# A hybrid encoder step on one core: low weight parts moved to VectorE, layer norm as two interleaved instructions a tile, output weights in pieces of 512

## The chip, the core and the metric

The kernel runs on one core of a Trainium2 chip. The metric is the device time of one execution in microseconds (us), taken as the median of several runs. Five engines work at once, each through its own instructions in a fixed order: TensorE (PE; its weight loads are PEld), VectorE (DVE), ScalarE (ACT), GpSimd (POOL) and SyncE (SP), which here issues the DMAs.

## What is computed

One layer of a streaming encoder for 2048 prompt tokens and 8 x 16 sample tokens (17 tiles of 128 tokens, 1024 features). All in float32, cut to what matters here:

```
h = RMSNorm(x);  u, v, zA, q, k, vv, zB, qi, ki, wi, gA, gB = split(h @ w_in)      # 1024 x 5704
vn   = LayerNorm(gelu(v)) * ln_g + ln_b                                             # 512 wide
a    = gelu(u) * (w_s @ vn + b_s) * silu(zA)                                        # per 128 tokens, 8 groups
score[q, l] = sum over 8 heads of relu(qi . ki) * wi;  keep the 256 best keys of each query
b    = softmax attention over the kept keys * silu(zB)
m    = sigmoid(gA) * (a @ w_pa) + sigmoid(gB) * (b @ w_pb)
y    = RMSNorm(x + m @ w_out)                                                       # 1024 x 1024
```

## The kernel before

Every matmul operand is held as two float32r numbers, a high part and a low part (`wh` and `wl`, `hh` and `hl`), and a product is three matmuls: high x high, high x low, low x high (`mm3`, line 170). The high part is made by ScalarE (`split_hi`, line 176), the low part, which is raw minus high, by `split_lo` (line 179) on the engine it is given.

**Weights.** `load_w` (line 140) brings a weight of 1024 rows and 128, 256 or 292 columns in chunks: SyncE issues a DMA into a staging tile `ws` (one buffer), ScalarE makes `wh`, GpSimd makes `wl` (one subtraction for the whole chunk: 128x1024, 128x512 or 128x1168), and the staging tile is free for the next DMA. `wh` and `wl` have two buffers, so one weight is prepared while the one before it is used. Only the very first weight has its low part made by VectorE.

**Order of the stages.** Tokens are worked on in two halves (9 tiles, then 8). `phase_p1` makes keys, values and queries; `phase_p2` makes mixer A: v in two pieces of 256 columns (`pairs`, gelu into `vn`), layer norm, u, the gate of mixer B, the spatial products (line 400) that read `vn`, and in the end the merge gates. Beside these the selection runs: `weave` takes steps of it between the steps of the main work. It has two lanes, each with its own query tile: `scores` (lines 504 to 511: two matmuls into a bank `ps_ix` of which there are two, ScalarE's relu into `r` with two buffers, VectorE's multiply-add into `s`), then 31 rounds of counting (line 581 on VectorE, line 591 on ScalarE) with small instructions on one number a partition (lines 592, 596, 597), then the mask (lines 623 to 632). This woven stage lies between about 245 us and 1445 us. Then `phase_b` is attention, and `phase_c` makes m and the output. Tile's scheduler fixes the order of each engine's instructions beforehand by its own simulated times; on the chip each engine keeps to it.

**Layer norm** (lines 371 to 385): after both pieces of v, per tile `bn_stats` and `bn_aggr` on VectorE; one Newton step for all tiles; then per tile one `tensor_scalar` on VectorE (line 381: minus mean, times factor) and two `tensor_tensor` on GpSimd (lines 382 and 383: times ln_g, plus ln_b).

**Output.** `phase_c` cuts `w_out` into four weights of 256 columns (`split_w`, tiles `wo0h` to `wo3l`), loaded in pieces while the first group is merged. `out` (line 987) makes a tile's 1024 columns as two banks of 512, and each bank as two sums of 24 matmuls with 256 moving columns (line 996).

Of the kernel before, what the change touches and what calls it, by code (L numbers as in the profile page):

```python
# [17 lines left out]
P = 128  # L18
# [39 lines left out]
def encoder_step(ctx: ExitStack, tc: tile.TileContext, x_prompt, x_sample, cache_k, cache_v, cache_kidx,  # L58
# [24 lines left out]
    class Banks:  # L83
        """PSUM, a bank a tile: how many banks each use has."""
# [30 lines left out]
    # scratch in DRAM  # L115
# [14 lines left out]
    def out_rows(prompt, sample, t, pat):  # L130
        """Token rows of tile t of an output [1, ...] as [128, width]."""
# [5 lines left out]
    # ---------------------------------------------------------------- weights  # L137
    WS_BUFS = 1

    def load_w(srcs, beside=False, eng=nc.gpsimd, stage=None):  # L140
        """Columns of weights as exact float32r pairs, [128, rows / 128, width] high and low: ranges of columns
        beside or below each other."""
# [5 lines left out]
        for below in ([srcs] if beside else [[s] for s in srcs]):  # L148
            n = below[0].shape[0] // P
            step = min(n, 1024 // width if width <= 256 else 4)  # L150
            for k in range(0, n, step):
# [9 lines left out]
                split_lo(wl[:, o], raw, wh[:, o], eng)  # L161
# [3 lines left out]
    def mm3(out, lh, ll, rh, rl, nk, cost):  # L165
        """Sum over nk of l[k]^T r[k] from float32r pairs, in steps."""
# [14 lines left out]
    def rsqrt(out, root, v):  # L181
        """1 / sqrt(v) from about sqrt(v), by a Newton step; root is lost."""
# [6 lines left out]
    def rms_scale(pool, x, out, g, inv=None, known=False, parts=1):  # L189
        """RMSNorm; inv keeps the factor."""  # L190
# [16 lines left out]
    # ---------------------------------------------------------------- phase A  # L207
# [5 lines left out]
    class Normed:  # L213
        """The transposed RMSNorm(x) of a half's tokens as float32r pairs, by group."""
# [5 lines left out]
        def ahead(self, n):  # L220
            """Loads and scales the rows of the next n tiles."""
# [48 lines left out]
    def phase_p1(half, hT, p1, wa, at_queries=None):  # L270
        """Keys, values, queries and the indexer's."""
        gs = HALVES[half]
        gids = [GROUP_OF[g[0]][0] for g in gs]
        # k | ki | wi | v
# [25 lines left out]
        for c, dst in ((C_QI, qi_s), (C_Q, q_s)):  # L300
            for b in range(2):
# [3 lines left out]
                for j in range(2):  # L305
                    for gid in gids:
# [3 lines left out]
                        sb = p1.tile([P, 512], F32, tag="ev", name="ev", bufs=3)  # L310
# [5 lines left out]

    def phase_p2(half, hT, at_gates=None):
        """Mixer A and its part of the merge; the gates of mixer B."""
# [832 lines left out]
```

## Time and profile before

| | |
|---|---|
| median of 3 runs | 2239.65 us (2237.88 to 2241.37) |
| profiled execution, span from first to last instruction | 2240.6 us (its own time is not listed apart from the runs) |
| PE busy | 2150.1 us, 96% |
| DVE busy | 1649.8 us, 74% |
| ACT busy | 1207.6 us, 54% |
| POOL busy | 567.2 us, 25% |
| chain that ended last | PE 63%, DVE 19%, DMA 6%, ACT 5% |

The profile is of one execution. Busy time counts an instruction from start to end; the matmuls of TensorE overlap each other, so its useful rate is read from the distance between starts, not from the busy share. The granted clock (PEclk) is a share of 2.4 GHz: 0.50 is the lower of its two levels, 1.2 GHz. "idle before" is time for which the engine had no instruction under way, with what ended it.

### The profile page before, as it was taken

The numbers are of one execution on the slowest core, as the hardware profiler recorded it, in microseconds if no ns is written. First come the engines' busy times: TensorE is split into PE (matmuls) and PEld (weight loads), VectorE is DVE, ScalarE is ACT, GpSimd is POOL, SyncE is SP. The second block draws the span as 40 slices with busy tenths as digits, with TensorE's granted clock in tenths as the row PEclk, the third lists the DMA queues.
The fourth block names the chain that finished last, engine by engine and source line by source line (L and its number), as shares of the span: only waits on it lengthen the run. The fifth ranks groups of instructions, "written<-read, shape, count | busy, mean of one in ns | idle before, by whom it ended". The sixth has DMA issues, their size and how long they took to land.

```text
span 2240.6 us, 39567 instructions
## 1 busy us (share of the span) xinstructions
PE 2150.1 (96%) x14712; PEld 2066.3 (92%) x14712; DVE 1649.8 (74%) x4034; ACT 1207.6 (54%) x2181; POOL 567.2 (25%) x437
## 2 busy tenths in 40 slices
PE   7999999899999999979998999999999999999998
PEld 7999999799999998979998999878899999989998
DVE  6205879998898897998988796578777788855343
ACT  5225646465565554545664654277766577743121
POOL 1121121432132121151123121132354423243000
PEclk9999999899999999999999999999999999999999
DMA  6333333123153233211223222553344421054341
GB/s 199 100 105 109 90 93 88 50 71 94 36 165 89 71 88 114 74 45 55 84 79 100 78 80 79 131 142 98 101 144 124 137 79 39 15 172 153 119 150 67
DMA packets 251008, 218.90 MB, mean 98 GB/s; under 512 B 46528, under 2 KB 238656, under 8 KB 250816
## 3 DMA queue, kind: packets, MB, share of 16 engines
q1 hardware_dynamic: 250816, 216.39, 32.7%
q8 instruction: 115, 1.88, 0.3%
q14 instruction: 77, 0.63, 0.1%
HBM read 152.45 MB, written 63.81 MB: 97 GB/s over the span
## 4 chain that ended last, share of the span: by engine, by line
PE 63%; DVE 19%; DMA 6%; ACT 5%; issue 4%; POOL 2%; SPq 1%; ACTq 0%; DVEq 0%; POOLq 0%
PE ps_mm L170 40%; DVE junk L581 5%; PE ps_po L747 5%; DVE s L511 4%; PE ps_tr L730 4%; PE ps_mm L706 2%; DVE bc L597 2%; PE ps_mm L707 2%; PE ps_ix L170 2%; ACT junk L591 2%; PE ps_ix L504 2%; PE ps_ix L505 1%; DMA ws<-in_w_in_dram 1%; DMA q<-q_s 1%; DVE vn L381 1%
## 5 line engine op out<-in xcount | busy, mean ns | idle before, releaser
L179 POOL TENSOR_TENSOR wl<-ws,wh 128x1024 fp32r<-128x1024 f32 (+1 forms) x102 | 238.5, 2338 | 951.8 <-ACT wh L176 928.5
L591 ACT ACTIVATE junk<-s,bc 128x384 int8<-128x384 f32 (+14 forms) x232 | 294.4, 1269 | 246.0 <-DVE bc L597 241.6
L170 PE MATMUL ps_mm<-wh,hh 128*128 128x256 f32 (+1 forms) x1360 | 393.0, 290 | 1.0 <-ACT vn L337 0.6
L170 PE MATMUL ps_mm<-wh,hl 128*128 128x256 f32 (+1 forms) x1360 | 393.1, 289 | 0.0
L170 PE MATMUL ps_mm<-wl,hh 128*128 128x256 f32 (+1 forms) x1360 | 392.2, 289 | 0.3 <-DVE wl L179 0.3
L170 PE MATMUL ps_mm<-hh,wh 128*128 128x384 f32 (+1 forms) x1152 | 379.5, 330 | 2.6 <-ACT ev L441 2.6
L170 PE MATMUL ps_mm<-hl,wh 128*128 128x384 f32 (+1 forms) x1152 | 378.7, 329 | 0.0
L170 PE MATMUL ps_mm<-hh,wl 128*128 128x384 f32 (+1 forms) x1152 | 376.8, 329 | 0.0
L581 DVE TENSOR_SCALAR_CACHE_REDUCE junk<-s,bc 128x512 int8<-128x512 f32 (+14 forms) x248 | 351.7, 1422 | 5.1
L170 PEld LDWEIGHTS ps_mm<-wh,hh 128*128 128x128 f32 x1360 | 260.5, 192 | 5.2 <-ACT hh L176 0.9
L170 PEld LDWEIGHTS ps_mm<-wl,hh 128*128 128x128 f32 x1360 | 261.1, 192 | 3.7 <-DVE wl L179 0.6
L170 PEld LDWEIGHTS ps_mm<-wh,hl 128*128 128x128 f32 x1360 | 260.6, 192 | 2.5 <-DVE hl L179 0.3
L511 DVE SCALAR_TENSOR_TENSOR s<-r,wiw,s 128x384 f32<-128x384 f32 (+2 forms) x266 | 230.7, 884 | 6.6 <-ACT r L507 6.0
L507 ACT ACTIVATE r<-ps_ix 128x512 f32<-128x512 f32 (+2 forms) x304 | 156.5, 537 | 138.0 <-DVE s L511 83.6
L170 PEld LDWEIGHTS ps_mm<-hh,wh 128*128 128x128 f32 x1152 | 217.6, 189 | 5.2 <-ACT ev L441 3.0
L170 PEld LDWEIGHTS ps_mm<-hh,wl 128*128 128x128 f32 x1152 | 217.4, 189 | 2.4 <-issue 0.4
L170 PEld LDWEIGHTS ps_mm<-hl,wh 128*128 128x128 f32 x1152 | 217.5, 189 | 1.5
L730 PE MATMUL ps_tr<-ident,sx 128*128 128x128 f32 x1088 | 170.1, 275 | 3.9 <-DVE ptl L179 1.7
L713 ACT ACTIVATE sx<-sx,mx 128x128 f32<-128x128 f32 (+15 forms) x128 | 153.8, 1203 | 25.2 <-DVE mx L712 25.0
L179 DVE TENSOR_TENSOR ptl<-ps_tr,pth 128x512 fp32r<-128x512 f32 (+1 forms) x231 | 149.9, 659 | 23.1 <-ACT pth L176 22.2
L176 ACT ACTIVATE pth<-ps_tr 128x512 fp32r<-128x512 f32 (+1 forms) x231 | 127.0, 572 | 63.7 <-PE ps_tr L730 59.0
L747 PE MATMUL ps_po<-pth,vst 128*128 128x256 f32 x544 | 156.6, 305 | 3.7 <-ACT osb L751 3.6
(306 smaller groups left out, 4936.7 us busy)
## 6 DMA issues: line engine op xcount, KB each, us to landing
ws<-in_w_in_dram SPq DMA_DIRECT2D x88, 512.0 KB, 3.9
x<-in_x_prompt_dram SPq DMA_DIRECT2D x41, 512.0 KB, 3.6
q<-q_s SPq DMA_DIRECT2D x34, 256.0 KB, 4.2
out_dram<-x SPq DMA_DIRECT2D x17, 512.0 KB, 2.6
gb_s<-ev SPq DMA_DIRECT2D x40, 192.0 KB, 1.9
ma_s<-ev SPq DMA_DIRECT2D x40, 192.0 KB, 1.9
ma<-ma_s SPq DMA_DIRECT2D x40, 192.0 KB, 3.2
sg<-gb_s SPq DMA_DIRECT2D x40, 192.0 KB, 2.9
```

Of the source, the lines that this page charges most:

```text
L170: nc.tensor.matmul(out, a(k), b(k), start=(n == 0), stop=(n == 3 * nk - 1))
L176: nc.scalar.activation(dst, src, AF.Copy)
L179: (eng or nc.vector).tensor_tensor(dst, src, hi.bitcast(F32), op=OP.subtract)
L504: nc.tensor.matmul(pi[:, :n], hi[:, h, :], kist[:, c:c + n], start=True, stop=False)
L507: nc.scalar.activation(r[:, :n], pi[:, :n], AF.Relu, scale=HD ** -0.5)
L511: nc.vector.scalar_tensor_tensor(s[:, c:c + n], r[:, :n], wiw[:, t, h:h + 1], s[:, c:c + n], op0=OP.mult, op1=OP.add)
L581: nc.vector.tensor_scalar(junk[:, :L], s[:, :L], thr, 0.0, op0=op, op1=OP.add, accum_out=cnt)
L591: nc.scalar.activation(junk[:, :L], s[:, :L], AF.Sign, bias=candf, scale=-1.0, accum_out=cnt)
L597: nc.vector.scalar_tensor_tensor(cand, g, (1 << b) >> 1, cand, op0=OP.bitwise_xor, op1=OP.bitwise_xor)
L713: nc.scalar.activation(sx, sx, AF.Exp, bias=mx[:, 7:8], scale=HD ** -0.5, accum_out=T.rsum[:, h:h + 1])
L730: nc.tensor.transpose(tv[:, l, hh * P:(hh + 1) * P], pr[hh][:, (l0 + l) * P:(l0 + l + 1) * P], ident)
L747: nc.tensor.matmul(po, vst[:, l0 + l, n, :], pp[:, l, :], start=(l0 + l == 0 and i == 0), stop=(l0 + l == t and i == 1))
```

## The change

The comments that went are left out. (1) `load_w` takes its engine from `LOW[0]`, which is GpSimd while the first half's `phase_p1` is traced and VectorE after that; the low part of a chunk is made in pieces of at most 512 columns (292 for the widths of 292), also for the first weight. (2) Layer norm: statistics of tile i are taken beside the products of the second piece of v, two tiles behind; the normalisation is two `scalar_tensor_tensor` a tile on VectorE, one step after each tile's products of the first piece of u, two steps a tile. `behind()` keeps each of them behind the VectorE instruction traced last. (3) `w_out` is held as two weights of 512 columns, and a bank is one sum of 24 matmuls with 512 moving columns. (4) Smaller: `r` has three buffers, and the mask's scan output `pre` takes one of them; `sel` shares the tile of `pen`; the gate's product on GpSimd is one instruction a tile (256 wide) where it was one for two tiles.

```
+    LOW = [nc.gpsimd]
-    def load_w(srcs, beside=False, eng=nc.gpsimd, stage=None):
+    def load_w(srcs, beside=False, eng=None, stage=None):
...
                 split_hi(wh[:, o], raw)
-                split_lo(wl[:, o], raw, wh[:, o], eng)
+                piece = max(1, 512 // width)
+                for j in range(0, step, piece):
+                    q = slice(k0 + k + j, k0 + k + j + piece)
+                    split_lo(wl[:, q], raw[:, j:j + piece], wh[:, q], eng or LOW[0])
...
+    def behind():
+        return tc.issue_after(next(i for i in reversed(nc.cur_bb.bb.instructions) if i.engine == mybir.EngineType.DVE))
...
-        def pairs(c, b, use):
+        def pairs(c, b, use, beside=None, of_beside=1):
...
                     yield from rows(hT, pm[:, j * 256:(j + 1) * 256], tiles[i + j], w, 0, 256)
+                    if beside:
+                        for _ in range(of_beside):
+                            next(beside, None)
...
+        def stats():
+            for i in range(-2, nt):
+                if i >= 0:
+                    nc.vector.bn_stats(st[:, i], vn[:, i])
+                    nc.vector.bn_aggr(mv[:, i], st[:, i])
+                yield
+        def normal():
+            for i in range(nt):
+                with behind():
+                    nc.vector.scalar_tensor_tensor(vn[:, i], vn[:, i], mv[:, i, 0:1], lgb[:, 0],
+                                                   op0=OP.subtract, op1=OP.mult)
+                yield
+                with behind():
+                    nc.vector.scalar_tensor_tensor(vn[:, i], vn[:, i], rs[:, 1, i:i + 1], lgb[:, 1],
+                                                   op0=OP.mult, op1=OP.add)
+                yield
...
-        for i in range(nt):
-            nc.vector.tensor_scalar(vn[:, i], vn[:, i], mv[:, i, 0:1], rs[:, 1, i:i + 1], op0=OP.subtract, op1=OP.mult)
-            nc.gpsimd.tensor_tensor(vn[:, i], vn[:, i], lgb[:, 0], op=OP.mult)
-            nc.gpsimd.tensor_tensor(vn[:, i], vn[:, i], lgb[:, 1], op=OP.add)
+        beside = normal()
...
-            yield from pairs(C_U, b, gelu_to(ug, 0))
+            yield from pairs(C_U, b, gelu_to(ug, 0), beside, 2)
             if b == 0:
+                for _ in beside:
+                    pass
...
-                nc.gpsimd.tensor_tensor(ug[:, i:i + m], ug[:, i:i + m], sb[:, :m], op=OP.mult)
+                for j in range(m):
+                    nc.gpsimd.tensor_tensor(ug[:, i + j], ug[:, i + j], sb[:, j], op=OP.mult)
...
-                r = tk.tile([P, 512], F32, tag="r", name="r", bufs=2)
+                r = tk.tile([P, 512], F32, tag="r", name="r", bufs=3)
...
-            pre = tk.tile([P, 512], F32, tag="pre", name="pre")
+            pre = tk.tile([P, 512], F32, tag="r", name="pre", bufs=3)
...
                 for c in range(2):
                     pm = bank("mm")
-                    for e in range(2):
-                        wh, wl = wo[2 * c + e]
-                        yield from mm3(pm[:, e * 256:(e + 1) * 256], lambda k: mh[:, k, i * P:(i + 1) * P],
-                                       lambda k: ml[:, k, i * P:(i + 1) * P], lambda k: wh[:, k, :],
-                                       lambda k: wl[:, k, :], KD, 2.6)
+                    wh, wl = wo[c]
+                    yield from mm3(pm, lambda k: mh[:, k, i * P:(i + 1) * P], lambda k: ml[:, k, i * P:(i + 1) * P],
+                                   lambda k: wh[:, k, :], lambda k: wl[:, k, :], KD, 5.2)
...
-    wa = load_w([cols(C_K), cols(C_KI, 36)], True, None, p1)
+    wa = load_w([cols(C_K), cols(C_KI, 36)], True, nc.vector, p1)
...
+    LOW[0] = nc.vector
     wa = load_w([cols(C_K), cols(C_KI, 36)], True)
```

## Rows read from the trace of the kernel before

**Rows 1.** The woven stage: us; PE, PEld, DVE, ACT, POOL busy us (instructions); clock; DMA.

```profile
245.00:1445.00 1200.00, 1152.28 (x7633) 1112.29 (x7632) 1018.90 (x2238) 660.91 (x1114) 304.29 (x175) 0.99 0.29 84
```

**Rows 2.** TensorE's waits from 245 to 1445 us: total, times, longest.

```profile
PE ps_ix L504 <- ACT r L507: 28.1, 21, 7.6
```

**Rows 3.** The same view by stretches: around the two layer norms.

```profile
425.00:445.00 20.00, 11.64 (x67) 10.49 (x68) 19.82 (x19) 4.47 (x9) 18.51 (x13) 0.75 0.11 30
956.00:986.00 30.00, 19.12 (x129) 18.05 (x128) 29.69 (x34) 8.80 (x18) 28.44 (x19) 0.89 0.07 18
```

**Rows 4.** Timeline of TensorE in the first: start, us, what, idle before.

```profile
439.90 0.80 PE L504 MATMUL ps_ix<-kist,qih 128*128 128x512 f32 x1 [7.60 <-ACT r L507]
```

**Rows 5.** Timeline of VectorE around both layer norms.

```profile
427.94 0.55 DVE L381 TENSOR_SCALAR vn<-vn,mv,rs 128x512 f32<-128x512 f32 x1
...
428.47 9.02 DVE L381 TENSOR_SCALAR vn<-vn,mv,rs 128x512 f32<-128x512 f32 x7
...
439.08 1.22 DVE L597 SCALAR_TENSOR_TENSOR bc<-bg,bc 128x1 int32<-128x1 int32 x1
...
955.33 0.75 DVE L511 SCALAR_TENSOR_TENSOR s<-r,wiw,s 128x512 f32<-128x512 f32 x1
```

**Rows 6.** Timeline of GpSimd in the first.

```profile
438.57 1.71 POOL L383 TENSOR_TENSOR vn<-vn,lgb 128x512 f32<-128x512 f32 x1
```

**Rows 7.** VectorE's groups, 245 to 1445 us: busy us, mean ns, idle before.

```profile
L597 DVE SCALAR_TENSOR_TENSOR bc<-bg,bc 128x1 int32<-128x1 int32 x433 | 126.0, 300 | 6.8
L511 DVE SCALAR_TENSOR_TENSOR s<-r,wiw,s 128x512 f32<-128x512 f32 x133 | 125.8, 959 | 4.0 <-ACT r L507 3.8
L511 DVE SCALAR_TENSOR_TENSOR s<-r,wiw,s 128x384 f32<-128x384 f32 x112 | 91.8, 829 | 2.3 <-ACT r L507 2.2
...
L592 DVE TENSOR_SCALAR bg<-bn 128x1 int32<-128x1 f32 x216 | 32.7, 151 | 124.8 <-ACT junk L591 123.3
...
L179 DVE TENSOR_TENSOR qi<-qi,qih 128x1024 fp32r<-128x1024 f32 x11 | 13.5, 1223 | 6.6 <-ACT qih L176 6.6
```

**Rows 8.** Line 597 over the whole span: shortest, median, longest ns.

```profile
L597 DVE SCALAR_TENSOR_TENSOR bc<-bg,bc x465: 120/159/2362, 210.6 to 1403.7; 128x1 int32<-128x1 int32 x155
```

**Rows 9.** GpSimd's groups over the whole span: busy us, mean ns.

```profile
L179 POOL TENSOR_TENSOR wl<-ws,wh 128x1024 fp32r<-128x1024 f32 x80 | 198.8, 2485 | 816.8 <-ACT wh L176 793.5 <-PE ps_ix L505 12.5 <-PE ps_ix L544 10.9
```

**Rows 10.** GpSimd's busy time on wl alone, then all engines' on vn alone, 245 to 1445.

```profile
245.00:1445.00 1200.00, 201.36 (x88) 0.99 0.29 84
...
245.00:1445.00 1200.00, 18.96 (x64) 11.03 (x64) 32.56 (x34) 10.04 (x18) 50.01 (x34) 0.99 0.29 84
```

**Rows 11.** Timeline of VectorE: a low part of 512 columns in phase C.

```profile
2032.64 0.68 DVE L179 TENSOR_TENSOR wo3l<-ws,wo3h 128x512 fp32r<-128x512 f32 x1
```

**Rows 12.** Timeline of VectorE: the last instruction of the selection.

```profile
1423.96 0.56 DVE L630 SCALAR_TENSOR_TENSOR pen<-junk,eq 128x384 bf16<-128x384 int8 x1
```

**Rows 13.** ScalarE's waits from 245 to 1445 us for staged weights.

```profile
ACT wh L176 <- DMA ws<-in_w_pa_dram: 18.2, 10, 5.8
ACT wh L176 <- DMA ws<-in_w_in_dram: 12.8, 10, 4.6
```

**Rows 14.** The chain that ended last, in order of time: start, us, what.

```profile
18.02 2.61 DVE inv L187
...
1294.44 144.71 PE ps_mm L170 x827
...
2037.51 194.80 PE ps_mm L170 x1620
```

**Rows 15.** Timeline of GpSimd at the start and in phase C.

```profile
17.14 3.48 POOL L179 TENSOR_TENSOR wl<-ws,wh 128x1168 fp32r<-128x1168 f32 x1 [15.83 <-ACT wh L176]
...
2039.54 1.29 POOL L179 TENSOR_TENSOR wo3l<-ws,wo3h 128x512 fp32r<-128x512 f32 x1 [1.21 <-ACT wo3h L176]
```

**Rows 16.** Timeline of TensorE: two matmuls of 512 moving columns in a row.

```profile
671.58 0.39 PE L504 MATMUL ps_ix<-kist,qih 128*128 128x512 f32 x1
671.80 0.39 PE L505 MATMUL ps_ix<-kist,qi 128*128 128x512 f32 x1
```

More of the change, by code (lines that the diff above doesn't have):

```diff
@@ L309, in phase_p1 @@
                         yield from feats(hT, pq[:, :n], gid, w, j * P)
-                        sb = p1.tile([P, 512], F32, tag="ev", name="ev", bufs=3)
+                        sb = p1.tile([P, 384], F32, tag="ev", name="ev", bufs=3)
                         nc.scalar.activation(sb[:, :n], pq[:, :n], AF.Copy)
@@ L368, in phase_p2 @@
         vn = p2.tile([P, nt, 512], F32, name="vn")
-        for b in range(2):
-            yield from pairs(C_V, b, gelu_to(vn, b * 256))
         st = p2.tile([P, 16, 6], F32, name="st")
         mv = p2.tile([P, 16, 2], F32, name="mv")
-        for i in range(nt):
-            nc.vector.bn_stats(st[:, i], vn[:, i])
-            nc.vector.bn_aggr(mv[:, i], st[:, i])
         rs = p2.tile([P, 3, 16], F32, name="rs")
+        def stats():
[14 more added lines that the diff above has]
+                yield
+            if half:
+                PS.dma_start(s_vn[0].rearrange("b s c -> (b s) c"), vn[:, nt - 1])
+        beside = stats()
+        for b in range(2):
+            yield from pairs(C_V, b, gelu_to(vn, b * 256), beside if b else None)
+        for _ in beside:
+            yield 0.4
         nc.scalar.activation(rs[:, 0, :nt], mv[:, :nt, 1], AF.Sqrt, bias=epsr[:, 1:2])
@@ L379, in phase_p2 @@
         rsqrt(rs[:, 1, :nt], rs[:, 0, :nt], rs[:, 2, :nt])
-        for i in range(nt):
-            nc.vector.tensor_scalar(vn[:, i], vn[:, i], mv[:, i, 0:1], rs[:, 1, i:i + 1], op0=OP.subtract, op1=OP.mult)
-            nc.gpsimd.tensor_tensor(vn[:, i], vn[:, i], lgb[:, 0], op=OP.mult)
-            nc.gpsimd.tensor_tensor(vn[:, i], vn[:, i], lgb[:, 1], op=OP.add)
-        if half:
-            PS.dma_start(s_vn[0].rearrange("b s c -> (b s) c"), vn[:, nt - 1])
+        beside = normal()
         at_s = {}
@@ L388, in phase_p2 @@
             ug = p2.tile([P, nt, 256], F32, tag="ug", name="ug")
-            yield from pairs(C_U, b, gelu_to(ug, 0))
+            yield from pairs(C_U, b, gelu_to(ug, 0), beside, 2)
             if b == 0:
+                for _ in beside:
+                    pass
                 yield from pairs(C_ZB, 0, gate_b)
@@ L531, in scores_sample @@
             BGL.dma_start(wh[h * DS:(h + 1) * DS], wv[h])
-        sel = tk.tile([P, 15 * DS], F32, tag="pre", name="sel")
+        sel = tk.tile([P, 15 * DS], F32, tag="pen", name="sel")
         nc.vector.memset(sel, 0.0)
@@ L540, in scores_sample @@
             nc.tensor.transpose(tp[:HD, PAST:LS], nk[:DS, b, :], ident[:DS, :DS])
-            kt = tk.tile([P, LS], F32, tag="r", name="kt", bufs=2)
+            kt = tk.tile([P, LS], F32, tag="r", name="kt", bufs=3)
             nc.vector.tensor_copy(kt[:HD], tp[:HD, :LS])
@@ L681, in encoder_step @@
     class Tile:
+        pass
     def attend_load(bp, t):
@@ L913, in attend_sample, with split_w @@
         bp.close()
-    def split_w(pool, src, nk, name, engs, bufs, after=None):
-        hi = pool.tile([P, nk, 256], F32R, name=name + "h")
-        lo = pool.tile([P, nk, 256], F32R, name=name + "l")
+    def split_w(pool, src, nk, name, engs, bufs, after=None, into=None):
+        hi, lo = into or [pool.tile([P, nk, 256], F32R, name=name + x) for x in "hl"]
         for i, k in enumerate(range(0, nk, 2)):
@@ L971, in use @@
                 if db in at:
-                    c = 256 * len(wo)
-                    wo.append(split_w(cp, w_out[0][:, c:c + 256], KD, f"wo{len(wo)}", (None, nc.gpsimd), 3,
-                                      mh.bitcast(F32)[:, db, 0:1]))
+                    c = 256 * at.index(db)
+                    if c % 512 == 0:
+                        wo.append([cp.tile([P, KD, 512], F32R, name=f"wo{len(wo)}{x}") for x in "hl"])
+                    split_w(cp, w_out[0][:, c:c + 256], KD, None, (None, nc.gpsimd), 3, mh.bitcast(F32)[:, db, 0:1],
+                            [w[:, :, c % 512:c % 512 + 256] for w in wo[-1]])
             return use
```

2 lines of the change are left out of this document (1 added, 1 removed).

## The prediction

> **What bounds the kernel now.** I read the page first: TensorE 96% busy, the others well below. Then the busy times by stage: in the woven stage (245 to 1445 us) TensorE is busy for 1152.28 of 1200 us and VectorE for 1018.90 [rows 1]. So TensorE's own rate sets the time there, and what a change can win is bounded by TensorE's idle time, 47.7 us, and by what the clock loses around it. The waits of TensorE say whose idle it is: 28.1 us before the score matmuls (line 504), which need a bank that ScalarE empties [rows 2]; a weight is nowhere among the long ones. The same view by stretches shows the place: 8.4 us idle of 20 at the first layer norm (425 to 445) and 10.9 of 30 at the second (956 to 986), together 19.2 us, at clocks of 0.75 and 0.89 on the mean [rows 3]. The timeline tells why: TensorE stands for 7.60 us before line 504 [rows 4] while VectorE runs seven line-381 instructions back to back, 9.02 us [rows 5]; the score's `r` can't be freed behind them, so ScalarE can't empty the bank. In the last stage the chain is TensorE alone, 1620 matmuls in 194.80 us [rows 14].
>
> One more thing has to be seen on VectorE. Line 381 takes 0.55 us alone and 9.02/7 = 1.29 us beside GpSimd; line 597, one number a partition, has a median of 159 ns and took 1.22 us when it met GpSimd's 1.71 us [rows 5, 6, 8]. Such a VectorE instruction stands until GpSimd's ends. In sum over the woven stage: line 597, 433 x (300 - 159) ns = 61 us; line 511, 133 x (959 - 750) = 28 us at 512 columns, and 112 x (829 - 610) = 25 us at 384 (610 being 750 less 128 columns of the slope below); line 381, 17 x 0.74 = 13 us [rows 5, 7, 8]. That is 127 us of VectorE's 1019 which is waiting and not work.
>
> **Low parts on VectorE.** From the second `phase_p1` on, 72 chunks of 128x1024, 16 of 128x512 and 4 of 128x1168 leave GpSimd (201.36 us for 88 of them [rows 10]; a chunk of 1024 took 2.485 us [rows 9]). A piece of 512 on VectorE costs 0.68 us [rows 11]; against 1.223 us for 1024 [rows 7] that is about 0.14 us fixed and 1.06 ns a column, so a piece of 292 costs 0.45. Added: (144 + 16) x 0.68 + 16 x 0.45 = 116 us. Layer norm adds 34 x 0.75 us = 25.5 us (line 511 is the same kind of instruction [rows 5]) and takes away 17 x 0.55 = 9.4: plus 16. What comes back is the waiting on GpSimd: `wl` and `vn` hold it for 201.36 + 50.01 of its 304.29 us [rows 1, 10], 83%, so 105 of the 127 us, or all 127 at best. Net VectorE is 5 to 27 us busier, 1046 of 1200 us at the most: not the bound. The chunk itself is ready sooner than before (two pieces 1.36 us against 2.485), but it now queues in order behind the selection, whose longest instructions are about two us; behind the low part stand the next DMA into the single staging tile on SyncE's queue, with the stores queued after it, and the matmuls of the next weight. That weight is due one weight later, 9 tiles x 24 matmuls x 120 ns = 26 us for two chunks, so a delay of a few us is covered. VectorE's new wait for ScalarE's high part, which waits for the DMA, is bounded by what ScalarE waits for that now, 18.2 + 12.8 = 31 us [rows 13], and below by nothing; behind it stand the selection's small instructions. VectorE has idle time for it: 123.3 us in which it waits for ScalarE's counts [rows 7]. The selection ends at 1424.5, the woven stage's matmuls at 1294.44 + 144.71 = 1439.2 [rows 12, 14]: 14.6 us of room. For all of this and the third `r` together I take -2 us; the bounds are -9 (the part of TensorE's 28.1 us at line 504 that lies outside the 19.2) and +12 (the waits use up the room and a third of what the lock gives back).
>
> By the Trainium skill, "SBUF — State Buffer", section "Who interferes with whom", a VectorE instruction with two SBUF inputs and a GpSimd instruction that reads SBUF exclude each other for the whole instruction, whoever starts first. The long rows agree; by that rule the moved low parts, which have two such inputs, can still be held up by what stays on GpSimd, 53 us of 1200, for which an estimate is some 5 us of VectorE, and the sum stands.
>
> **Layer norm.** The burst goes: two instructions of 0.75 us follow each tile's products of 24 x 120 ns = 2.9 us, and statistics go beside v. Clean, the two stretches give back 19.2 us of idle less 1.2 us of ordinary idle (28.5 us over the other 1150 us, for 50 us), plus what was done at the lower clock: a mean of 0.75 over 20 us and 0.89 over 30 us is 10 and 6.6 us at 1.2 GHz, most of it the idle itself; I take 4 us for the rest. Together 22. VectorE was at 19.82 of 20 us there [rows 3] and keeps most of that work, and each inserted instruction can delay a score by 0.75 us, so I take 18 of 22; bounds 8 and 24. The products that read `vn` come a gate of mixer B later, some 25 us: a late layer norm is covered. The gate's halves on GpSimd cost a fixed part more, hidden by its 75% of idle.
>
> **Output weights.** 1632 matmuls of 256 become 816 of 512. The spacing at 256 is 194.80 us / 1620 = 120.2 ns and at 384 it is 144.71 / 827 = 175.0 [rows 14]; the slope gives 230 ns at 512, and one pair of starts gives 220 (to 10 ns) [rows 16]. Saved per pair 10.4 ns, in all 8.5 us, all on the path. Against it: a bank of the second half now wants both its weights with the first matmul, where the last quarter came 24 matmuls (2.9 us) later, and the last low part ends at 2040.8 [rows 15]; plus 1. Net -7.5, bounds -14 and -1.
>
> By the Trainium skill, "TensorE: Matmul & The Clock Gate", section "Wait — 56ns, not 53.3ns?", the fixed part of a warm matmul is about 2.5 ns, by which the pairs would save 2 us and the sum would be smaller by 6.5. The rows show some 13 ns at 256 columns (120.2 against 256 columns at 2.4 GHz), so I keep 8.5.
>
> **Start.** VectorE stands 2.61 us in one small instruction (line 187) behind GpSimd's 3.48 us low part [rows 14, 15]; in quarters it stands at most 0.87, so -1.6; the first weight's two chunks in quarters cost 2 x 3 x 0.14 = 0.9 more. Net -0.7, bounds -2 and +1.
>
> **Sum.** -2 - 18 - 7.5 - 0.7 = -28.2. The profiled span, 2240.6, is 0.95 us above the median of the runs, so I apply the sum to both: 2212.4 of span, 2211.5 of time.
>
> **The rivals.**
> - *The burst only moves* (chance 0.20). VectorE is full in that stretch before and after; the scores wait just as long, a little later, and of 22 us only 4 come back. For it: 99% busy there [rows 3], and the total of VectorE's work does not shrink. Against: the seven in a row were what stood before one score. 2239.65 - 7.5 - 0.7 - 2 - 4 = 2225.
> - *VectorE becomes the bound of the woven stage* (0.13, slower). 132 us of work are added; if the lock gives back little and the idle of 123.3 us (two lanes in lockstep) can't be filled since low parts wait in order for ScalarE, the selection outlasts the matmuls. Later by 132 - R - F - 14.6, R being what comes back and F the idle that is filled; the other terms give 26, so it is slower from R + F below 91 us. With R + F = 60 it ends 57 us late and the time is 2239.65 + 57 - 26 = 2271. Against: R alone should be 105.
> - *It does not do what it says* (0.08, same). The scheduler's simulated order still puts the layer norm's instructions together, and weights of the second half hold the output by as much as the width wins: -18 goes, -7.5 goes, leaving 2237.
> - The forecast has 0.59.
>
> **Range and chances.** The forecast's bounds are -14 - 24 - 2 - 9 = -49 and -1 - 8 + 1 + 12 = +4, so 2191 to 2244; I give 2192 to 2243, which holds the second and fourth case too and leaves out most of the slower one. 0.2% is 4.5 us, about what a measurement of this kernel can tell from no change. Faster: 0.59 + 0.20 = 0.79; same 0.08; slower 0.13.
>
> **What would show it.** Line 597's mean falls from 300 to under 200 ns in the woven stage, line 511's at 512 to under 800. `wl` is a VectorE row of 0.68 us, x160, and GpSimd's busy time there falls to about 60 us. TensorE has no idle over 3 us at a layer norm and the clock stays above 0.95 there; its idle before line 504 falls from 28 to about 12 us. No wait of TensorE for `wl` of more than a us; if such waits stand high on its list, the low parts come too late and the second rival has begun. The output rows read 128x512, x816 in all, with starts 230 ns apart; at 240 that term is nothing. The selection's last line 630 lies ahead of the last merge matmul; if it lies behind, VectorE is the bound.

## The result and the profile after

The changed kernel takes 2270.64 us (median of 4 runs, 2267.12 to 2273.45); the kernel before, run beside it, 2240.51 (2237.88 to 2243.56). The ratio is 1.0136, 95% interval 1.0120 to 1.0153: slower, where I forecast 2211 and faster. The profiled execution's span is 2265.3 us against 2240.6.

The page of the kernel after: busy times, and the lines of TensorE and its clock in 40 slices of 56.6 us each.

```profile
PE 2158.3 (95%) x13896; PEld 2025.6 (89%) x13896; DVE 1627.2 (72%) x4233; ACT 1221.5 (54%) x2181; POOL 315.4 (14%) x341
...
PE   8999999999999999995799999979999999999998
...
PEclk9999999999999999995799999979999999999999
```

One hole stands out, two slices from about 1020 to 1130 us. The view by windows shows it: the whole woven stage (the answer to [rows 1]), then 430 to 505 us, where the first layer norm is now, and the hole (columns as in [rows 1]).

```profile
245.00:1445.00 1200.00, 1145.26 (x7490) 1092.43 (x7489) 970.60 (x2367) 667.17 (x1101) 57.31 (x59) 0.96 0.27 80
430.00:505.00 75.00, 70.53 (x521) 65.65 (x520) 65.49 (x180) 41.32 (x68) 4.29 (x7) 0.95 0.23 68
1010.00:1087.00 77.00, 41.13 (x104) 23.52 (x103) 65.59 (x127) 40.42 (x68) 0.00 (x0) 0.59 0.08 21
```

The same 77 us of the kernel before:

```profile
1010.00:1087.00 77.00, 76.10 (x587) 73.24 (x587) 66.27 (x124) 46.11 (x70) 16.47 (x9) 1.00 0.22 64
```

104 matmuls stand where 587 stood, so some 63 us of TensorE's work (483 of 587 times 77) are missing; part of it is had back elsewhere. Who is waited for: TensorE's waits from 245 to 1470 us (total, times, longest), then the timeline of VectorE and TensorE in and before the hole (start, us, what, idle before).

```profile
PE ps_tr L432 <- DVE vn L401: 17.0, 2, 15.0
PE ps_ix L537 <- ACT qih L181: 13.2, 3, 6.0
PE ps_ix L537 <- ACT r L540: 9.4, 15, 1.3
```

```profile
921.30 0.16 DVE L413 TENSOR_SCALAR rs<-mv 128x9 f32<-128x9 f32 x1
...
922.35 0.17 DVE L192 TENSOR_TENSOR rs<-rs 128x9 f32<-128x9 f32 x1
...
1053.30 0.75 DVE L397 SCALAR_TENSOR_TENSOR vn<-vn,mv,lgb 128x512 f32<-128x512 f32 x1
...
1090.08 0.74 DVE L401 SCALAR_TENSOR_TENSOR vn<-vn,rs,lgb 128x512 f32<-128x512 f32 x1
```

```profile
1086.84 2.07 PE L432 MATMUL ps_tr<-vn,wst 128*128 128x512 f32 x2 [14.99 <-DVE vn L401]
```

The layer norm's factors are there at 922.5. Its first instruction (line 397) starts 131 us later and its last (line 401) ends at 1090.8; the spatial products (line 432, 400 before) need `vn`, and in TensorE's fixed order only score matmuls stand before them. VectorE is not full meanwhile: 65.59 of 77 us. The layer norm waits because `behind()` ties each of its instructions behind the VectorE instruction that was traced last before it, which is one of the selection; whether this makes the hole is tested below.

The groups that the forecast had named, VectorE from 245 to 1445 us (busy us, mean ns | idle before), answering [rows 7, 11]:

```profile
L184 DVE TENSOR_TENSOR wl<-ws,wh 128x512 fp32r<-128x512 f32 x160 | 106.3, 699 | 32.3 <-ACT wh L181 31.5 <-issue 0.3
L544 DVE SCALAR_TENSOR_TENSOR s<-r,wiw,s 128x512 f32<-128x512 f32 x133 | 104.7, 802 | 23.2 <-ACT r L540 22.7
L544 DVE SCALAR_TENSOR_TENSOR s<-r,wiw,s 128x384 f32<-128x384 f32 x112 | 68.6, 628 | 13.8 <-ACT r L540 13.4
L630 DVE SCALAR_TENSOR_TENSOR bc<-bg,bc 128x1 int32<-128x1 int32 x431 | 67.9, 168 | 5.6
```

Most of the waiting on GpSimd is gone (300 to 168 ns for line 597, now 630), as forecast. The output matmuls start 226 ns apart (timeline of TensorE):

```profile
2149.80 0.39 PE L175 MATMUL ps_mm<-wo0l,mh 128*128 128x512 f32 x1
2150.03 0.39 PE L175 MATMUL ps_mm<-wo0h,ml 128*128 128x512 f32 x1
2150.25 0.39 PE L175 MATMUL ps_mm<-wo0h,mh 128*128 128x512 f32 x1
```

To compare kernels I cut the span at two places: the first matmul of the attention's logits and the first output matmul. Both are in the rows of one line or tile (count, shortest/median/longest ns, first and last start); before, then after:

```profile
L706 PE MATMUL ps_mm<-kst,qh x320: 279/396/667, 1449.9 to 1961.1; 128*128 128x512 f32 x92, 128*128 128x384 f32 x60, 128*128 128x128 f32 x4, 128*128 128x256 f32 x4
L170 PE MATMUL ps_mm<-wo0h,mh x136: 279/283/535, 2018.9 to 2223.1; 128*128 128x256 f32 x136
```

```profile
L739 PE MATMUL ps_mm<-kst,qh x320: 278/397/596, 1477.0 to 1991.9; 128*128 128x512 f32 x92, 128*128 128x384 f32 x60, 128*128 128x128 f32 x4, 128*128 128x256 f32 x4
L175 PE MATMUL ps_mm<-wo0h,mh x136: 387/389/632, 2050.6 to 2250.2; 128*128 128x512 f32 x136
L663 DVE SCALAR_TENSOR_TENSOR pen<-junk,eq x39: 279/684/1505, 272.2 to 1469.4; 128x512 bf16<-128x512 int8 x28, 128x384 bf16<-128x384 int8 x4, 128x128 bf16<-128x128 int8 x3, 128x256 bf16<-128x256 int8 x3
```

The last row is the masks: the selection now ends at 1470, where it ended at 1424.5 [rows 12]. Until the attention it takes 1477.0 us (before 1449.9), from there to the output 573.6 (569.0), and the rest 214.7 (221.7). So the loss is 27 us in the woven stage and 5 in the attention, and the gain of 7 us in the output is as forecast.

### The profile page after: what moved, and what is told of

The parts are those of the page before. It is cut to its first block, busy times and chain, and to the rows that moved or that the text cites. A ratio compares the mean times of both kernels' runs of the same rounds, so it can differ in the third digit from the quotient of the medians.

```text
span 2265.3 us, 38034 instructions
## 1 busy us (share of the span) xinstructions
PE 2158.3 (95%) x13896; PEld 2025.6 (89%) x13896; DVE 1627.2 (72%) x4233; ACT 1221.5 (54%) x2181; POOL 315.4 (14%) x341
## 4 chain that ended last, share of the span: by engine, by line
PE 80%; DVE 7%; DMA 5%; ACT 3%; issue 2%; SPq 1%; POOL 1%; ACTq 0%; DVEq 0%; POOLq 0%
PE ps_mm L175 56%; PE ps_po L780 5%; PE ps_tr L763 4%; PE ps_ix L537 2%; PE ps_mm L739 2%; PE ps_ix L538 2%; PE ps_mm L740 2%; PE ps_ix L175 2%; DVE junk L614 2%; DMA ws<-in_w_in_dram 1%; DMA q<-q_s 1%; PE ps_mm L791 1%; DVE s L544 1%; DMA qi<-qi_s 1%; DMA x<-in_x_prompt_dram 1%
## 5 line engine op out<-in xcount | busy, mean ns | idle before, releaser
L544 DVE SCALAR_TENSOR_TENSOR s<-r,wiw,s 128x384 f32<-128x384 f32 (+2 forms) x266 | 184.2, 713 | 37.3 <-ACT r L540 36.1
L184 DVE TENSOR_TENSOR wl<-ws,wh 128x512 fp32r<-128x512 f32 (+1 forms) x184 | 115.8, 668 | 72.5 <-ACT wh L181 71.7
L181 ACT ACTIVATE wh<-ws 128x1024 fp32r<-128x1024 f32 (+1 forms) x104 | 104.1, 1001 | 102.0 <-DMA ws<-in_w_in_dram 59.2
```

What stands on the lines that cost most here:

```text
L181: nc.scalar.activation(dst, src, AF.Copy)
L184: (eng or nc.vector).tensor_tensor(dst, src, hi.bitcast(F32), op=OP.subtract)
L544: nc.vector.scalar_tensor_tensor(s[:, c:c + n], r[:, :n], wiw[:, t, h:h + 1], s[:, c:c + n], op0=OP.mult, op1=OP.add)
```

## The experiments

Four theories were set against each other, A and B before the first runs, C and D after them. **A**: the tie makes the loss, by the hole above. **B**: VectorE's low parts make it. **C**: the selection, which is a chain of VectorE and ScalarE and runs on into the attention when it is late, sets a pace of its own, and what TensorE wins in the woven stage is given back there. **D**: the third buffer of `r`, which is shared with the masks' prefix sums `pre`, ties the selection's two lanes to each other; D1 says that the sharing does it, D2 the third buffer as such. (In the expectations of the two runs with fewer rounds, D stands for something else, which is told there.) All times below are medians; ratios are to the kernel before, run beside each.

**One part alone, and the change without the tie.** Without the tie:

```
     def behind():
-        return tc.issue_after(next(i for i in reversed(nc.cur_bb.bb.instructions) if i.engine == mybir.EngineType.DVE))
+        return nullcontext()
```

> The changed kernel with one thing taken out: the layer norm's instructions are no longer tied behind the VectorE instruction traced last. Theory A (the tie): in the second half the selection runs some 120 us behind the place at which it is traced, the tied instructions start at 1053 us though their factors are there at 922, and TensorE runs dry from 1010 to 1087. Without the tie they run when their factors are there, as a burst, and about 60 of the 67 us come back: 2210 us (2200 to 2225). Theory B (VectorE is the bound of the woven stage with 116 us of low parts more, and layer norm is late because VectorE is full): nothing much comes back, 2255 us or more.

Measured: 2248.98, ratio 1.0041 (1.0026 to 1.0056). The layer norm's first instructions of the second half start from 889.1 to 914.8 us, and the hole is filled (the row of line 397, then the window of the hole, both of the change without the tie):

```profile
L397 DVE SCALAR_TENSOR_TENSOR vn<-vn,mv,lgb x9: 733/745/747, 889.1 to 914.8; 128x512 f32<-128x512 f32 x9
```

```profile
1010.00:1087.00 77.00, 77.00 (x581) 73.69 (x580) 46.39 (x86) 42.98 (x71) 1.47 (x2) 1.00 0.21 62
```

A is shown for the hole, but only 21.7 us come back; the time lies in neither theory's range, and the kernel still isn't faster than before. Where the rest went stands in the rows that cut the span, and in the masks' row:

```profile
L739 PE MATMUL ps_mm<-kst,qh x320: 278/402/792, 1399.8 to 1971.7; 128*128 128x512 f32 x92, 128*128 128x384 f32 x60, 128*128 128x128 f32 x4, 128*128 128x256 f32 x4
L175 PE MATMUL ps_mm<-wo0h,mh x136: 389/389/628, 2033.6 to 2229.5; 128*128 128x512 f32 x136
L663 DVE SCALAR_TENSOR_TENSOR pen<-junk,eq x39: 284/684/919, 270.8 to 1609.2; 128x512 bf16<-128x512 int8 x28, 128x384 bf16<-128x384 int8 x4, 128x128 bf16<-128x128 int8 x3, 128x256 bf16<-128x256 int8 x3
```

The attention begins 50 us earlier than before (1399.8) and takes 633.8 us instead of 569.0, with masks until 1609: the woven stage's gain is given back. Beside the masks VectorE is nearly full, 106.42 us of 110 from 1500 to 1610 where it was 89.77 before (windows of the attention in the kernel before, then in this one; columns as in [rows 1]):

```profile
1500.00:1610.00 110.00, 107.08 (x755) 96.69 (x754) 89.77 (x303) 84.88 (x192) 31.17 (x34) 0.98 0.35 94
1500.00:1610.00 110.00, 96.73 (x651) 82.22 (x649) 106.42 (x305) 80.52 (x150) 24.07 (x26) 0.98 0.21 56
```

The kernel before with the new layer norm, statistics beside v and tie included (the edit shortened):

```
-        nc.gpsimd.tensor_tensor(vn[:, i], vn[:, i], lgb[:, 0], op=OP.mult) ...
+        with behind(): nc.vector.scalar_tensor_tensor(vn[:, i], vn[:, i], mv[:, i, 0:1], lgb[:, 0], ...)
```

> The kernel before with the new layer norm alone (statistics beside v, two tied VectorE instructions a tile); low parts stay on GpSimd, the output weights at 256. Theory A: the selection is as far behind its traced place as in the changed kernel or further, since GpSimd still holds VectorE up; TensorE runs dry before the products that read vn in the second half: 2265 to 2300 us. Theory B: without the low parts VectorE has room, layer norm comes in time and the two stalls of some 20 us go: 2215 to 2240 us.

Measured: 2251.53, ratio 1.0046 (1.0027 to 1.0065). The same without the tie (`behind()` as in the first diff):

> The kernel before with the new layer norm alone and without the tie: two VectorE instructions a tile, placed by the scheduler. Theory A: the dry stretch of the tied form (30 us from 1050 to 1100) goes, 2225 to 2240 us, against 2251 with the tie. If the tie was not the cause of that stretch: 2250 us again.

Measured: 2227.57, ratio 0.9948 (0.9931 to 0.9966). The tie turns a gain of 11.5 us into a loss of 10.8: it costs 22 to 24 us here too. Both theories had missed the first of the two runs (A 2265 or more, B 2240 or less); the second came out as A said.

The kernel before with the low parts on VectorE, in pieces of 512 (the edit shortened):

```
-                split_lo(wl[:, o], raw, wh[:, o], eng)
+                for j in range(0, step, piece):
...
+                    split_lo(wl[:, q], raw[:, j:j + piece], wh[:, q], eng or LOW[0])
...
+    LOW[0] = nc.vector
```

> The kernel before with the low parts on VectorE in pieces of 512 alone. Theory A: low parts are not what costs; VectorE's waiting behind GpSimd goes and TensorE's small waits before line 504 shrink: 2215 to 2238 us. Theory B: VectorE is the bound, the selection outlasts the matmuls of the woven stage: 2255 us or more.

Measured: 2255.08, ratio 1.0066 (1.0050 to 1.0081). In its trace the attention begins at 1426.7 us, 23 earlier than before, but takes 600.4 us, 31 more, and the last mask is at 1502.7 (before 1424.0). The time fits B (2255 or more), and the rows read as C has it; for this part alone C was not tested.

The kernel before with `w_out` in pieces of 512 (shortened; the tiles are made 512 wide as in the change):

```
-                    for e in range(2):
-                        wh, wl = wo[2 * c + e]
+                    wh, wl = wo[c]
```

> The kernel before with the output weights in pieces of 512 alone. Both theories: the term of the prediction, -7.5 us (the last stage from the first output matmul to the last one is 7.6 us shorter in the changed kernel): 2232 us (2228 to 2236).

Measured: 2235.83, ratio 0.9974 (0.9964 to 0.9984): a gain of 4.9 us.

**Does the selection set the pace?** The change without the tie, and the kernel before, each with 27 instead of 31 rounds of counting:

```
-        for b in range(30, -1, -1):
+        for b in range(30, 3, -1):
```

> The changed kernel without the tie, and with 27 of the 31 counting rounds of the selection (the last four bits of the threshold are left out). Theory C (new): the selection's two lanes are the pace of the woven stage. Without the tie TensorE's merge matmuls end at 1387 us, 52 earlier than before, but the selection goes on into the attention and slows it, whose stage is 65 us longer; the gain is given back. Four rounds less of 31 take some 100 us off the selection, it ends with the matmuls again, and the 2249 us without the tie fall by 40 to 60: 2190 to 2210 us. Theory D (the attention is slower for another reason: its loads, its place in memory, its bank pool): little changes, 2240 us or more.

> The kernel before with 27 of the 31 counting rounds (the last four bits of the threshold are left out). Theory C: before, the selection ended at 1424 us and the matmuls at 1439, so it held nothing up at the end; only a few of TensorE's waits shrink: 2220 to 2240 us, far less than the changed kernel without the tie wins by the same cut. Theory D: the same 0 to -10 us as there.

Measured: 2213.91 for the first, 35 us under the same with all rounds; 2242.18 for the second, ratio 1.0008 (0.9993 to 1.0023). Work taken from the selection is worth 35 us in the one kernel and nothing in the other. So C is shown for the change without the tie: before, the selection was covered by the matmuls, and there it isn't. The gain is less than the 40 to 60 expected, since the shortened selection still ends late: its last mask is at 1512.0, 123 us after the attention began (1389.3).

**What makes it late?** First the low parts, back on GpSimd but in pieces of 512, in the change without the tie:

```
-    LOW[0] = nc.vector
```

> The changed kernel without the tie, and with the low parts on GpSimd to the end (in pieces of 512). Theory C with the low parts as what makes the selection longer (some 80 us in the run of the low parts alone): the selection ends near 1430 us, 2215 to 2235 us. If the low parts do not matter for the selection (the waits behind GpSimd cost it as much): 2243 to 2255 us.

Measured: 2242.27, ratio 1.0017 (1.0003 to 1.0031): 7 us less, and the last mask still near 1541 us. So B does not explain most of the lateness. What this kernel has beyond the untied layer norm alone (2227.57) is `w_out`, which gains, the smaller pieces, and the buffers of `r`. The buffers, alone in the kernel before (`sel` in the tile of `pen`, and the samples' tiles that share the rotation, go with them, as in the change):

```
-                r = tk.tile([P, 512], F32, tag="r", name="r", bufs=2)
+                r = tk.tile([P, 512], F32, tag="r", name="r", bufs=3)
...
-            pre = tk.tile([P, 512], F32, tag="pre", name="pre")
+            pre = tk.tile([P, 512], F32, tag="r", name="pre", bufs=3)
```

> The kernel before with the third buffer of r alone (the mask's prefix sums among them, the sample's selector in the penalty's buffer). Theory D: the last mask moves from 1424 to 1450 or later, and the time rises by 5 to 12, to 2245 to 2252. Rival: within 2 us of the kernel before, last mask at 1410 to 1430, because the woven stage has room for a buffer more or less. My prediction's own step had a gain of up to 5 here from relus that no longer wait for a buffer: 2235 to 2240.

Measured: 2278.67, ratio 1.0178 (1.0162 to 1.0193). This part alone costs 38.7 us, more than the whole change and far more than the 5 to 12 expected. Line 507 makes the `r` tiles; its rows from 895 to 1003 us, of the kernel before and then with the third buffer, and ScalarE's timeline in the latter:

```profile
L507 ACT ACTIVATE r<-ps_ix x34: 468/534/618, 906.3 to 999.3; 128x512 f32<-128x512 f32 x17, 128x384 f32<-128x384 f32 x17
```

```profile
L507 ACT ACTIVATE r<-ps_ix x8: 483/540/599, 933.1 to 1001.9; 128x512 f32<-128x512 f32 x4, 128x384 f32<-128x384 f32 x4
```

```profile
935.44 0.60 ACT L507 ACTIVATE r<-ps_ix 128x512 f32<-128x512 f32 x1 [1.77 <-DVE eq L628]
...
995.13 0.86 ACT L507 ACTIVATE r<-ps_ix 128x384 f32<-128x384 f32 x2
...
999.85 1.09 ACT L507 ACTIVATE r<-ps_ix 128x512 f32<-128x512 f32 x2 [3.37 <-DVE eq L628]
```

Line 628 is the last reader of `pre`. In this stretch one lane scores the tile of 1792 keys and the other selects for the samples. With `pre` in the rotation the next score tiles have their place behind the other lane's mask: 8 relus are begun by 1002 us where 34 were. The some 60 us without a relu (936 to 995) are not made up, and it is not the only such pause: from 1116 to 1183 us none begins either until line 628 has run. The last relu of line 507 begins at 1366.8 us (before 1294.5), the masks end at 1564 (1424), and the attention takes 617 us instead of 569; what lengthens the selection further after its last relu was not taken apart:

```profile
L706 PE MATMUL ps_mm<-kst,qh x320: 278/398/775, 1441.1 to 2001.0; 128*128 128x512 f32 x92, 128*128 128x384 f32 x60, 128*128 128x128 f32 x4, 128*128 128x256 f32 x4
L170 PE MATMUL ps_mm<-wo0h,mh x136: 278/283/356, 2058.3 to 2259.1; 128*128 128x256 f32 x136
L630 DVE SCALAR_TENSOR_TENSOR pen<-junk,eq x39: 286/685/2735, 270.2 to 1564.1; 128x512 bf16<-128x512 int8 x28, 128x384 bf16<-128x384 int8 x4, 128x128 bf16<-128x128 int8 x3, 128x256 bf16<-128x256 int8 x3
```

The opposite: the change without the tie and with two buffers of `r` and `pre` on its own (the last diff undone, `sel` included, on top of the first).

> The change without the tie, and with two buffers of r and a buffer of its own for the mask's prefix sums, as the kernel before has them. Theory D (the shared third buffer couples the two lanes: the masks' prefix sums of one lane wait for score tiles of the other, and so the selection ends at 1609 instead of 1424): the last mask comes 50 us or more earlier and the time falls by 8 to 15, to 2234 to 2241. Rival (the selection is late because of the low parts on VectorE and because TensorE's denser matmuls push its score matmuls back): the time stays within 3 us of 2249 and the last mask comes after 1560.

Measured: 2211.51 (2209.23 to 2217.09), ratio 0.9882 (0.9863 to 0.9901), 37.5 us under the change without the tie. This is the version to keep: 59 us faster than the change as it was made, 28 faster than the kernel before.

```profile
L739 PE MATMUL ps_mm<-kst,qh x320: 277/415/562, 1405.0 to 1937.2; 128*128 128x512 f32 x92, 128*128 128x384 f32 x60, 128*128 128x128 f32 x4, 128*128 128x256 f32 x4
L175 PE MATMUL ps_mm<-wo0h,mh x136: 389/389/628, 1997.0 to 2194.8; 128*128 128x512 f32 x136
L663 DVE SCALAR_TENSOR_TENSOR pen<-junk,eq x39: 289/684/1577, 272.2 to 1485.2; 128x512 bf16<-128x512 int8 x28, 128x384 bf16<-128x384 int8 x4, 128x128 bf16<-128x128 int8 x3, 128x256 bf16<-128x256 int8 x3
```

The gain is far above the 8 to 15 expected. The attention begins 45 us earlier than before and takes 592.0 us, 23 more; the output takes 212.4, 9 less.

The kernel before with the untied layer norm and `w_out` together:

> The kernel before with two parts of the change: the layer norm as two VectorE instructions a tile without the tie, and w_out in pieces of 512. Low parts stay on GpSimd in pieces of one row block, two buffers of r. If the parts lie in different stages (layer norm in the woven stage, output weights in the last one) their gains add: 2227.6 (layer norm untied alone) and 4.7 less from w_out alone, so about 2222, and the last output stage about 7 us shorter than before. If the selection is what limits (theory C), the gain of the last stage still stands whole, since no selection runs there: also 2222. If both gains rest on the same slack: 2227.

Measured: 2221.08, ratio 0.9921 (0.9904 to 0.9938): 18.9 us, against 11.5 and 4.9 alone. They add, within the noise: the product of the two ratios is 0.9922.

**What was still open.** The changed kernel with its tie, but two buffers of `r`:

> The changed kernel with its tie, but two buffers of r and a buffer of its own for the masks' prefix sums. Without the tie the same undoing took 37.5 us off. If sharing and tie cost the same stretch only once (both push the selection's and the tied instructions' place together, the selection's lateness being what the tie multiplies), the time falls from 2270.6 to 2235 to 2248 and TensorE's dry stretch at 1050 to 1087 shrinks; if the parts add, to 2233. Rival: the tie is what decides here and the time stays at 2260 or more.

Measured: 2256.27, ratio 1.0071 (1.0052 to 1.0090). So the tie costs 44.8 us where the buffers are not shared (2256.27 against 2211.51) and 21.7 where they are; the sharing costs 37.5 without the tie and 14.4 with it. Together they cost 59.1, less than the 82.3 of each by itself, and the time lies in neither of the two expected ranges. As the rows read, the matmuls that the hole makes late cover the late selection: with both, the last mask is at 1469.4 and the attention begins at 1477.0; with the sharing alone it is 1609.2 against 1399.8. What the sharing still costs beside the tie is a longer hole: the last line 401 starts at 1090.1 us with it and at 1069.0 without.

Low parts on GpSimd in pieces of 512, no tie, two buffers of `r`:

> The change without the tie, two buffers of r, masks' prefix sums apart, and the low parts on GpSimd in pieces of 512: against the one with the low parts on VectorE (2211.5) it shows that part's sign once the shared buffer is gone. If VectorE's 15 to 20 us of low parts lengthen the selection as they did with the shared buffer (by 7), the time is 2203 to 2206. If the low parts on VectorE are a gain because no lock on the port holds them up and weights come sooner (2221.1 for layer norm and w_out alone speaks for it), 2217 to 2222.

Measured: 2216.16, ratio 0.9896 (0.9881 to 0.9911). With nothing else in the way the low parts on VectorE take 4.7 us off by the medians and 3 by the ratios, whose intervals overlap: a gain is not shown, and a loss as in the run of the low parts alone (14) is not there. The attention begins at 1405.0 instead of 1423.3 and takes 592.0 instead of 580.4. It is the trade of the kernel with the low parts alone (-23, +31), at another price. Why the price differs isn't settled.

Three buffers of `r`, but `pre` on its own; to make room, masks in pieces of 384. In the kernel before, then in the change without the tie (the edit is the second's, shortened; the first also gets the third buffer, and `sel` in the tile of `pen`):

```
-            pre = tk.tile([P, 512], F32, tag="r", name="pre", bufs=3)
+            pre = tk.tile([P, 384], F32, tag="pre", name="pre")
```

> The kernel before with three buffers of r for the scores, and the masks' prefix sums in a buffer of their own; to make the room, masks are built in pieces of 384 columns (up to 2 more pieces a tile, some 1 us of VectorE each). Theory D1 (the sharing does the harm: a prefix sum in the rotation lets no score tile of the other lane past until the mask is done): 2238 to 2250, last mask at 1415 to 1440, scores of the tile with 1792 columns under way from 915 on without the pause from 939 to 1000. D2 (a third buffer as such changes the order of relus and counts): 2265 or more and the pause is there.

> The change without the tie, three buffers of r, the masks' prefix sums in a buffer of their own in pieces of 384. D1: within 6 us of the one with two buffers (2211.5), on either side: 2206 to 2218. D2: 2240 or more.

Measured: 2263.11, ratio 1.0100 (1.0082 to 1.0118), and 2214.86, ratio 0.9894 (0.9877 to 0.9912). And the smaller pieces, with `sel` in the tile of `pen` and two buffers:

> The kernel before with masks in pieces of 384 columns and the sample's selector in the penalty's buffer, two buffers of r: the control for the kernel with the third buffer and prefix sums apart (2263.1). If the pieces cost what their extra instructions are worth (some 14 more pieces in all, 1 to 1.5 us of VectorE each, beside other work): 2240 to 2250, and the third buffer as such costs 13 to 23. If the smaller pieces reorder the selection and cost the whole 22: 2258 or more, and the third buffer as such costs nothing.

Measured: 2250.46, ratio 1.0048 (1.0033 to 1.0062). In the first of the three the pause is gone: the tile of 1792 keys is scored from 930 to 1000 us without such a stop, and the last mask is at 1428.8. D1 is right about what delays the selection, and its time (2238 to 2250) did not come: 22.6 us are lost all the same, 10.0 by the pieces and `sel`, and so 12.6 by the third buffer itself, spread over small idle times of TensorE (the attention begins at 1464.4 instead of 1453.3 with the pieces alone). So of the 38.7 us some 26 are the sharing, if the parts add, which no run shows. In the change without the tie pieces and third buffer together cost 3.3 us, which the noise could make, so there the sharing makes up nearly all of the 37.5. A third buffer gains nothing in either, and why it costs more in the one isn't settled.

## Why the prediction was wrong

**The low parts, the waiting on GpSimd and the third buffer (-2, bounds -9 and +12).** This is the first of two terms that failed, and it failed by the words "and the third `r` together": I gave the third buffer no price of its own. The diff also moves `pre` into that rotation, so that a score tile of one lane waits for the mask of the other. Third buffer and sharing cost 38.7 us in the kernel before, three times the upper bound of the whole term, and 37.5 in the change without the tie. The rest of the term held: line 597's mean fell to 168 ns, `wl` is a row of 699 ns, x160, TensorE never waited for a weight's low part in the woven stage, and GpSimd's busy time fell to 57.31 us. VectorE's time came back as estimated: 431 x 132 ns = 57 us on line 630, and on line 544 at 512 columns 133 x 157 ns = 21 us and on its 384s 112 x 201 ns = 23 us, so about 100 of the 105 us. (By the slope that the forecast used, the 384s alone take 614 ns and not 610; half a us in the sum.) With two buffers and no tie, the low parts on VectorE cost nothing that can be told from noise.

**Layer norm (-18, bounds -24 and -8).** The size was within its bounds: untied and alone it gave 11.5 us, two thirds of it. The step that failed is "a late layer norm is covered" by some 25 us, and beside two buffers of `r` it is the dearer of the two failures: 44.8 us. I took the tied instruction's place to be the place of its products in the code. The tie gives it the place of a selection instruction, and the selection runs behind the place at which it was traced, the further the later: in the first half the layer norm begins 38 us after its factors are ready, in the second 131. For the first half in the kernel after, the last step of the factors and the row of line 397:

```profile
L192 DVE TENSOR_TENSOR rs<-rs x1: 161/161/161, 414.4 to 414.4; 128x8 f32<-128x8 f32 x1
...
L397 DVE SCALAR_TENSOR_TENSOR vn<-vn,mv,lgb x8: 745/747/750, 452.7 to 490.9; 128x512 f32<-128x512 f32 x8
```

The 38 us were covered but for a few us of idle (70.53 of 75 us busy from 430 to 505). In the second half TensorE had other work until 1010, 88 us after the factors, so more than I had reckoned, and the layer norm ended at 1090.8. I had never asked how far the selection lags. The clock at the first layer norm was 0.95, as forecast; in the hole it was 0.59.

**"Not the bound".** VectorE's load in the woven stage was right (970.60 us after, with part of the selection moved out of the window), and the conclusion was wrong. The 14.6 us of room between the selection's end and the matmuls' end was not room for the change: each us by which TensorE gets faster takes one from it. The forecast gave TensorE some 20 us and left the selection where it was. In the kernel as changed the hole hides this; without the tie it shows. In the best version the last mask comes 80 us after the attention began, and the attention takes 23 of the 45 us won in the woven stage. That the selection takes them there too is argued from the same picture; a run with fewer rounds was made only with the shared buffer.

**The second rival came out right in its number, and not in its reason.** It said 2271 and 2270.6 was measured, but its condition was R + F below 91 us, and R alone is about 100. In the kernel as changed VectorE was not full; the selection was late since its score tiles stood behind masks, and the layer norm was late since it stood behind the selection. The sign that I had named for this rival did come: the last mask, at 1469.4, lies 4 us behind the end of the merge matmuls, and its penalty's load is in the chain that ended last (in order of time, the kernel after).

```profile
1328.53 137.25 PE ps_mm L175 x784
1474.14 5.22 DMA penx<-pen_s
```

But that cost next to nothing here: the attention begins 11.2 us after the merge matmuls end (1465.8 to 1477.0), and before it was 10.7. Another sign, no idle over 3 us at a layer norm, failed by the 15.0 us before line 432, and that one was the loss.

**The output weights (-7.5, bounds -14 and -1).** From the first output matmul to the end 221.7 us became 214.7; alone the part gave 4.9. The spacing at 512 columns is 226 ns against a forecast of 230 from the slope. By the Trainium skill, "TensorE: Matmul & The Clock Gate", section "Wait — 56ns, not 53.3ns?", a warm matmul has a fixed part of about 2.5 ns, so an estimate by it is that a pair saves that much; the rows give 2 x 120.2 - 226 = 14.4 ns a pair, and the measurement decides. That makes 816 x 14.4 ns = 11.7 us, of which 7.0 came. The bank that now wants both weights waits 3.9 us once, where before TensorE waited 1.8 for `wo2h` and 0.7 for `wo3l`: 1.4 more, and I had 1 (TensorE's waits in the output, after, then before). Where the other 3 us went isn't settled.

```profile
PE ps_mm L175 <- ACT wo1h L181: 3.9, 1, 3.9
```

```profile
PE ps_mm L170 <- ACT wo2h L176: 1.8, 1, 1.8
...
PE ps_mm L170 <- DVE wo3l L179: 0.7, 1, 0.7
```

**The sum.** With the two causes taken out the kernel takes 2211.5 us, and I forecast 2211. That is partly luck: the layer norm gave 11.5 for 18 and the output 4.9 for 7.5, and what is left, 28.4 - 18.9 = 9.5 us, is for the low parts and the smaller pieces, for which I had 2.7.

## What to carry to other kernels

A tile that joins a rotation of buffers is an edit with a price of its own: list all that shares the rotation, how long each holds its buffer, and whether two chains of work that were independent now wait for each other. Before an instruction is tied behind another one, look in the trace for the time at which that other one runs, not for its place in the code. And where a background chain ends just under the cover of the main engine, what the main engine wins is not won until that chain is shorter too: cut the chain a little in both kernels and see which of them moves.

## What was not expected of the hardware

The hole has a second price that I had not put on any step, a small one. While TensorE had only score matmuls now and then, the granted clock fell to its lower level (1.2 GHz): the window 1010 to 1087 us shows 0.59 on the mean. The second matmul of a score pair, which stands right behind the first, takes 0.40 us at 512 columns ahead of the hole and 0.63 in it (timeline of TensorE in the kernel after, then two windows of the same kernel).

```profile
1004.24 0.40 PE L538 MATMUL ps_ix<-kist,qi 128*128 128x512 f32 x1
...
1060.40 0.63 PE L538 MATMUL ps_ix<-kist,qi 128*128 128x512 f32 x1
```

```profile
1095.00:1105.00 10.00, 7.88 (x20) 3.97 (x19) 9.92 (x24) 6.07 (x8) 4.18 (x6) 0.50 0.01 2
1105.00:1115.00 10.00, 10.00 (x72) 10.00 (x71) 8.22 (x25) 7.81 (x13) 2.15 (x4) 0.80 0.16 54
```

The windows show that the first products after the hole are still done at 0.50, and that the clock comes back in the 10 us after them. In TensorE's timeline some 25 products of 256 columns start 0.21 us apart from 1103.6 to 1108.9 us, and from there 0.12: an estimate of the price is 25 x 0.09 = 2 us, besides the spatial products before them.
